# A hybrid encoder layer on one core: the first rows loaded ahead of the constants and whole, u's first product in a bank of its own, the final norm's products shared by VectorE and GpSimd

## The chip, the core and the metric

The kernel runs on one core of one Trainium2 chip. The core has five engines with a queue of instructions each: TensorE (PE in the profile, its weight loads PEld), VectorE (DVE), ScalarE (ACT), GpSimd (POOL) and SyncE (SP), which here issues all transfers between memory and the core. The metric is the device time of one execution in microseconds; the median of a few runs is given.

## What is computed

One layer of an encoder over two sequences of 512 tokens and 1024 features (a prompt and a sample), each with a memory of 256 rows of its own. Cut to what matters here:

```
def _layer(x, mem, l, p):
    xn = _rmsnorm(x, p['norm_mix'][l])
    mn = _rmsnorm(mem, p['norm_mem'][l])
    h = xn @ p['w_in'][l]
    u, q, k, v, xq, g = jnp.split(h, IN_SPLITS, axis=-1)
    y_s5 = _s5_branch(u, ...)
    ...
    y_diff = _diff_attention(q, k, v, lam, ...)
    mk, mv = jnp.split(mn @ p['w_mem_kv'][l], 2, axis=-1)
    y_x = _cross_attention(xq, mk, mv)
    ...
    x = x + merged @ p['w_out'][l]
    xn2 = _rmsnorm(x, p['norm_ffn'][l])
    gate, up = jnp.split(xn2 @ p['w_ffn_in'][l], 2, axis=-1)
    return x + (jax.nn.silu(gate) * up) @ p['w_ffn_out'][l]

def _trunk(x, mem, p):
    for l in range(DEPTH):
        x = _layer(x, mem, l, p)
    return _rmsnorm(x, p['norm_final'])
```

DEPTH is 1. The change touches three places: the first step of `mn @ w_mem_kv`, the first columns of `h` (which are `u`, the input of the state-space branch), and the last `_rmsnorm` with `norm_final`.

## The kernel before

Features lie on the 128 partitions, tokens along the free axis: both sequences together are 1024 columns, and 1024 features are 8 blocks (KD) of 128. Every matrix product in full precision is made of three: weight and data are each split into a high part (a rounded copy, made by ACT) and a low part (the rest, made by DVE), and `mm3` multiplies high by high, high by low and low by high into one bank (L134 to L138 are `split`, the products themselves are all recorded at L66). `weight` loads one 128x1024 weight tile `wf` (L146) and splits it into `wh`, `wl`; each of these three tiles has two buffers.

PE writes its sums to banks of 512 columns. There are eight: four in the pool `mm`, taken with `bank()`, and four in the pool `tr`, taken with `aux()`. A bank is given out again in turn, once its last reader is done.

**Start.** The constants `vec` (the scales of all the norms) are loaded first (L118). `NWARM` products of zeros keep PE busy until the first data are there. Then comes the memory product: `w_mk[0]` is loaded in two halves, each split on arrival, and behind each half `mem_part(i)` loads and splits a part of the memory, two blocks of features at a time (`mh`, `ml`, `mt` in the rows; the norm's scale out of `vec` goes in with the split, L137 and L138). Part 0 is loaded in two transfers, one per block (L228), the others in one (L225). `mem_k(h, w)` makes a quarter of the memory's keys, `mem_v(c, w)` a quarter of its values, the values of all four quarters being summed in four banks `ob` of the pool `mm`. Between them ACT and DVE prepare the layer's input: sums of squares, the norm's factor (`factor`: square root on ACT, reciprocal on DVE, then a transpose on PE that spreads the factor over a bank `bc`), and `x_norm`, which makes `xh`, `xl`.

**u.** After `mem_v(3)` the four banks `ob` are copied by ACT (L371, `mf` in the rows). The first product of u takes the next bank of the same pool, which is the first of these four.

**End.** The last 4 of the 22 blocks of the second feed-forward product are done for three groups of columns: all 512 of the first sequence (c = 0), then the first and the second 256 of the other (c = L and c = L + L // 2). For each group and each of the 8 blocks m of features PE makes the product, DVE adds it to `y[m]` (L1315), ACT squares it, and the squares are added up. `final` then takes the norm's factor and scales the 8 blocks: on DVE in one instruction with the scale `norm_final` and the factor read from its bank (L1292), or, for the middle group, on POOL (L1290), which gets the factor as a copy that ACT makes (`b_`, L1287, `acc` in the rows), the scale having been put in by ACT before (L1319). `final` yields after each block, and for the middle group its steps are called between the blocks of the last group. After each two blocks the result is stored (L1295).

The text's order isn't the order of a queue: the library that builds the program places the instructions of each engine itself, within their dependencies. `issue_after(x)` is a tie: what stands in it comes behind instruction x on the same engine.

Of the kernel before, what the change touches and what calls it, by code (L numbers as in the profile page):

```python
# [10 lines left out]
F32 = mybir.dt.float32  # L11
F32R = mybir.dt.float32r
I32 = mybir.dt.int32
AF = mybir.ActivationFunctionType
ALU = mybir.AluOpType
# [4 lines left out]
P = 128  # L20
L = 512
DM = 1024
KD = DM // P
NS = 2
NT = NS * L
# [47 lines left out]
def encoder(ctx: ExitStack, tc: tile.TileContext, a, out):  # L73
    nc = tc.nc
    V, S, PO, PE = nc.vector, nc.scalar, nc.gpsimd, InOrder(tc, nc.tensor)
# [7 lines left out]
    wp = ctx.enter_context(tc.tile_pool(name="wp", bufs=2))  # L83
# [22 lines left out]
    def slot(tag, shape=(P, NT), dt=F32, name="sl"):  # L106
        return pools[tag].tile(list(shape), dt, tag=tag, name=name)

    def bank(tag="mm"):
        return pools[tag].tile([P, 512], F32, tag=tag, name="bk" + tag)  # L110

    def aux():
        return bank("tr")


    ident = cst.tile([P, P], F32, name="ident")
    vec = cst.tile([P, N_VEC], F32, name="vec")
    nc.sync.dma_start(vec, a["vecs"])  # L118
    onec = cst.tile([P, 2], F32, name="onec")
    V.memset(onec, 1.0)  # L120
# [5 lines left out]
    def vcol(name, i=0):  # L126
        o = VEC[name][0] + i
        return vec[:, o : o + 1]


    def split(hi, lo, src, scale=None):

        if scale is None:
            h = S.copy(hi, src)  # L134
            l_ = V.tensor_tensor(out=lo, in0=src, in1=hi.bitcast(F32), op=ALU.subtract)  # L135
        else:
            h = S.activation(out=hi, in_=src, func=AF.Copy, scale=scale)  # L137
            l_ = V.scalar_tensor_tensor(out=lo, in0=src, scalar=scale, in1=hi.bitcast(F32), op0=ALU.mult, op1=ALU.subtract)  # L138
        return h, l_
# [3 lines left out]
    def weight(src, n=DM, tag=None):  # L143
        nonlocal last_w, last_s
        wf = wp.tile([P, DM], F32, tag="wf", name="wf")
        last_w = nc.sync.dma_start(wf[:, :n], src)  # L146
        wh, wl = (slot(tag, dt=F32R, name=n_) if tag else wp.tile([P, DM], F32R, tag=n_, name=n_) for n_ in ("wh", "wl"))
        last_s = split(wh[:, :n], wl[:, :n], wf[:, :n])
        return wh, wl
# [3 lines left out]
    def mm3(outs, wh, wl, xs, k, nk):  # L153

        nonlocal last_mm
        ws = slice(k * P, (k + 1) * P)
        for s, (xh, xl) in enumerate(xs):
            PE.matmul(outs[s], wh[:, ws], xh, start=(k == 0), stop=False)
            PE.matmul(outs[s], wh[:, ws], xl, start=False, stop=False)
        for s, (xh, xl) in enumerate(xs):  # L160
            last_mm = PE.matmul(outs[s], wl[:, ws], xh, start=False, stop=(k == nk - 1))
# [33 lines left out]
    def factor(ss, n, nt=4, bias=epsc):  # L195

        rs = rp.tile([P, 4], F32, tag="rs", name="rs", bufs=4)
        S.activation(out=rs[:, :nt], in_=ss[:, :nt], func=AF.Sqrt, scale=1.0 / n, bias=bias)
        V.reciprocal(rs[:, :nt], rs[:, :nt])
        bc = aux()  # L200
        for t in range(nt):
            PE.transpose(bc[:, t * P : (t + 1) * P], rs[:, t : t + 1].broadcast_to([P, P]), ident)
        return rs, bc
# [16 lines left out]
    ml = [slot("it" if i else "mem", [P, 2, L], F32R, f"ml{i}") for i in range(4)]  # L220

    def mem_part(i):
        mt_ = slot("ld", [P, 2, L], name="mt")
        if i:
            nc.sync.dma_start(mt_, a["memT"][:, 2 * i : 2 * i + 2, :])  # L225
        for j in range(2):
            if i == 0:
                nc.sync.dma_start(mt_[:, j], a["memT"][:, j, :])  # L228
            split(mh[i][:, j, :], ml[i][:, j, :], mt_[:, j, :], scale=vcol("norm_mem", 2 * i + j))

    last_sq = None
# [62 lines left out]
    def queued():  # L294

        return tc.issue_after(last_w.ins)
# [9 lines left out]
    for _ in range(NWARM):  # L306
        PE.matmul(idle[:, :P], pad_r[:, :P], pad_r[:, :P], start=True, stop=True)


    wf = wp.tile([P, DM], F32, tag="wf", name="wf")  # L310
    wh, wl = (wp.tile([P, DM], F32R, tag=n_, name=n_) for n_ in ("wh", "wl"))
    for i in range(2):
        hs = slice(i * L, (i + 1) * L)
        nc.sync.dma_start(wf[:, hs], a["w_mk"][0][:, hs])
        split(wh[:, hs], wl[:, hs], wf[:, hs])
        mem_part(i)
    mw = [(wh, wl)]
    mem_part(2)
    mem_part(3)
    mw.append(weight(a["w_mk"][1]))  # L320
    with queued():
# [29 lines left out]
    with yielding(last_s):  # L351
        x_norm(0, norm[0], range(5, 8))
        _, bc = factor(ss1, DM)
# [12 lines left out]
    with tc.issue_after(last_s[0].ins):  # L366
        mfs = []
        for s in range(NS):
            mfs.append(slot("ld", [P, 2, L], name="mf"))
            for j in range(2):  # L370
                S.copy(mfs[s][:, j], ob[2 * s + j])  # L371
    uw.append(weight(a["w_in"][1]))
    with queued():
        next(s5)
    for s in range(NS):
# [8 lines left out]
    for t2 in range(2):  # L384
        if t2:
            uw = [weight(a["w_in"][2 + t]) for t in range(2)]
        us = [slot("ld", [P, T, NS, NC], name="ut") for _ in range(2)]
        for s in range(NS):
            for t in range(2):
                o = bank()  # L390
                for k in range(KD):
                    mm3([o], *uw[t], [x_of(k, s)], k, KD)
                S.copy(us[t][:, :, s, :], o.rearrange("p (j c) -> p j c", c=NC))
        for t in range(2):
            nc.sync.dma_start(uD[(2 * t2 + t) * P : (2 * t2 + t + 1) * P], us[t])
# [121 lines left out]
    with behind():  # L517
# [3 lines left out]
        rs_, bc = factor(sums(a["memN"], "ld"), DM)  # L521
# [4 lines left out]
    for t in range(4):  # L526
        o = proj(a["w_glu"][t], zh, zl, 4)
# [37 lines left out]
    ld = lp.tile([P, 2], F32, tag="ld", name="ld", bufs=1)  # L565
# [9 lines left out]
    for i in range(4):  # L575
        th, tl = slot("mkv", [P, 2, L], F32R, "mkvh"), slot("mkv", [P, 2, L], F32R, "mkvl")
        mt_ = slot("ld", [P, 2, L], name="mt")
# [108 lines left out]
    for i in range(-AHEAD, len(steps) + 1):  # L686
        if i + AHEAD < len(steps):
            h, s, lt = steps[i + AHEAD]
# [12 lines left out]
        if 0 <= i < len(steps):  # L701
            h, s, lt = steps[i]
# [8 lines left out]
        if i > 0 and steps[i - 1][2] == 3:  # L711
            h, s, _ = steps[i - 1]
            pTh, pTl = pT.pop((h, s))
            oo = bank("oo")
            hs = slice(h * P, (h + 1) * P)
# [109 lines left out]
    s0, ss, osb = {}, {}, {}  # L825
# [72 lines left out]
    n = len(steps)  # L898
# [226 lines left out]
    for i in range(KFF):  # L1125
# [16 lines left out]
        if i == 0:  # L1142
            for s in range(NS):
                _, bc = rstd(accs[s], DM)
# [3 lines left out]
        with ExitStack() as es_:  # L1148
# [3 lines left out]
            for s, gf, up in ((0, gf0, up0), (1, gf1, up1)):  # L1152
                cs = slice(s * L, (s + 1) * L)
# [17 lines left out]
    y = [y2[m // 2][:, m % 2] for m in range(KD)]  # L1171
# [46 lines left out]
    for v, (m, lo_, hi_) in enumerate(VISITS):  # L1218
        ps = [bank() for _ in range(6)] + [aux()]
        for p in range(lo_, hi_):  # L1220
# [12 lines left out]
            for p_, (nm, o) in zip(ps, SEVEN):  # L1233
                wh, wl = w[nm]
# [40 lines left out]
    def column_sums(acc, n):  # L1275
        ss = aux()
        ones(ss, acc, n, True, True)
        return ss

    def final(ss, c0, n):  # L1280

        cs = slice(c0, c0 + n)
        _, bc = factor(ss, DM, n // P)
        if c0 == L:

            b_ = new_acc()
            S.copy(b_[:, :n], bc[:, :n])  # L1287
        for m in range(KD):
            if c0 == L:
                PO.tensor_tensor(out=y[m][:, cs], in0=y[m][:, cs], in1=b_[:, :n], op=ALU.mult)  # L1290
            else:
                V.scalar_tensor_tensor(out=y[m][:, cs], in0=y[m][:, cs], scalar=vcol("norm_final", m), in1=bc[:, :n],  # L1292
                                       op0=ALU.mult, op1=ALU.mult)
            if m % 2 == 1:
                nc.sync.dma_start(out[c0 // L, :, m - 1 : m + 1, c0 % L : c0 % L + n], y2[m // 2][:, :, cs])  # L1295
            yield
# [3 lines left out]
    for c, n in ((0, L), (L, L // 2), (L + L // 2, L // 2)):  # L1300
        acc = new_acc()
        for m in range(KD):
            if c == 0:
                wsrc = a["w_fo"][m, :, 2 * NPAIR * P :]
                if m == 0:
                    kept.append(weight(wsrc, nb * P))
                else:
                    wf = wp.tile([P, DM], F32, tag="wf", name="wf")[:, : nb * P]
                    nc.sync.dma_start(wf, wsrc)
                    split(k0[:, m - 1], k1[:, m - 1], wf)  # L1310
                    kept.append((k0[:, m - 1], k1[:, m - 1]))
            o = bank()[:, :n]
            for k in range(nb):
                mm3([o], *kept[m], [(ah[k][:, c : c + n], al[k][:, c : c + n])], k, nb)
            V.tensor_tensor(out=y[m][:, c : c + n], in0=y[m][:, c : c + n], in1=o, op=ALU.add)  # L1315
            if c + n < NT or m < KD - 3:
                sum_sq(acc, y[m][:, c : c + n], m == 0, n, V if m == KD - 1 else PO)
                if c == L:
                    S.activation(out=y[m][:, c : c + n], in_=y[m][:, c : c + n], func=AF.Copy, scale=vcol("norm_final", m))  # L1319
                elif c > L:  # L1320
                    for _ in range((0, 0, 1, 2, 5)[m]):
                        next(end)
                continue

            if m == KD - 3:
                ss = aux()
                ones(ss, acc, n, start=True)
            sq = rp.tile([P, L], F32, tag="nsq", name="nsq", bufs=2)
            S.square(sq[:, :n], y[m][:, c : c + n])
            ones(ss, sq, n, stop=(m == KD - 1))  # L1330
        end = final(ss if c + n == NT else column_sums(acc, n), c, n)
        if c != L:
            for _ in end:
                pass
# [422 lines left out]
```

## Time and profile before

| | us |
|---|---|
| median of three runs (lowest, highest) | 1606.04 (1605.71, 1608.06) |
| the profiled execution | 1609.13 |
| its span | 1607.4 |
| PE busy | 1587.6 (99%) |
| DVE busy | 1164.2 (72%) |
| ACT busy | 638.6 (40%) |
| POOL busy | 560.7 (35%) |
| mean granted clock of PE | 0.998 |

The page and the queries show one profiled execution. A row of the order in time reads: start, duration, engine, line, operation, output <- inputs, shapes, number of instructions merged, and in brackets how long the engine was idle before and who released it. "SPq" is SP's issue of a transfer, not the transfer itself. Rows of waits read: who waited, for whom, microseconds in total, times, the longest. `bkmm` and `bktr` are banks of the two pools. Where rows of a GB/s line are shown, the window is cut into 40 equal slices.

### The profile page before, as it was taken

Reading aid. Unit: us, or ns where it says so; the run is one execution under the profiler, and the core shown is the slowest. Engines: PE = TensorE matmul, PEld = TensorE weight load, DVE = VectorE, ACT = ScalarE, POOL = GpSimd, SP = SyncE. Lnnn points to the kernel's source line nnn. Section 1 sums busy time; section 2 is a strip of 40 time slices with the busy share of each in tenths; the row PEclk is TensorE's granted clock in tenths of the full one; section 3 lists DMA queues with packets and bytes.
Section 4 is the critical chain, followed back from the end, with each engine's and each line's share of the span. In section 5 each row is a group of like instructions: output and inputs, shape, how many; then the busy total and the mean of one; then the engine's idle time right before and its main releaser. Section 6 shows DMA issues by size and latency. Waiting matters only on the chain.

```text
span 1607.4 us, 21636 instructions
## 1 busy us (share of the span) xinstructions
PE 1587.6 (99%) x7842; PEld 1314.0 (82%) x7842; DVE 1164.2 (72%) x1853; ACT 638.6 (40%) x1142; POOL 560.7 (35%) x452
## 2 busy tenths in 40 slices
PE   9999999999999999999999999999999999999997
PEld 7888788887898779777878887888888888788887
DVE  7976997067774666766454668888889877898764
ACT  6644313265552355564123434233323233233333
POOL 0010100000333221300343367666656655644563
PEclk9999999999999999999999999999999999999999
DMA  9544523676763111135354532333332223885322
GB/s 357 179 158 151 166 100 123 178 259 211 255 222 112 41 59 40 58 131 176 134 184 137 153 103 90 125 120 131 118 117 107 92 79 128 325 333 187 107 66 105
DMA packets 105035, 237.86 MB, mean 148 GB/s; under 512 B 13536, under 2 KB 45024, under 8 KB 104928
## 3 DMA queue, kind: packets, MB, share of 16 engines
q1 hardware_dynamic: 104928, 236.47, 43.2%
q8 instruction: 62, 1.02, 0.3%
q14 instruction: 45, 0.37, 0.1%
HBM read 165.16 MB, written 71.27 MB: 147 GB/s over the span
## 4 chain that ended last, share of the span: by engine, by line
PE 85%; DVE 4%; issue 4%; DMA 3%; POOL 3%; ACT 1%; SPq 0%; DVEq 0%; POOLq 0%; ACTq 0%
PE bkmm L66 73%; PE bktr L66 2%; PE bksc L66 2%; PE bkoo L66 2%; PE bktr L69 2%; DMA yt<-bD 1%; PE bktr L1591 1%; POOL mg L788 1%; POOL ts L964 1%; DVE tl L135 1%; POOL y L1244 1%; PE bktr L1562 1%; PE bktr L1651 0%; PE bktr L1650 0%; PE bktr L1652 0%
## 5 line engine op out<-in xcount | busy, mean ns | idle before, releaser
L66 PE MATMUL bkmm<-xh,wh 128*128 128x512 f32 x640 | 255.7, 399 | 0.9 <-ACT mf L371 0.9
L66 PE MATMUL bkmm<-xh,wl 128*128 128x512 f32 x640 | 250.7, 392 | 0.0
L66 PE MATMUL bkmm<-xl,wh 128*128 128x512 f32 x640 | 250.5, 391 | 0.0
L66 PE MATMUL bkmm<-th,wh 128*128 128x512 f32 (+1 forms) x621 | 241.1, 388 | 0.7 <-ACT th L134 0.7
L66 PE MATMUL bkmm<-tl,wh 128*128 128x512 f32 (+1 forms) x621 | 241.2, 388 | 0.6 <-DVE tl L135 0.6
L66 PE MATMUL bkmm<-th,wl 128*128 128x512 f32 (+1 forms) x621 | 240.8, 388 | 0.0
L134 ACT CAST wh<-wf 128x1024 fp32r<-128x1024 f32 (+1 forms) x134 | 117.8, 879 | 185.3 <-PE bkmm L66 162.7
L135 DVE TENSOR_TENSOR wl<-wf,wh 128x1024 fp32r<-128x1024 f32 (+1 forms) x134 | 148.9, 1111 | 51.7 <-ACT wh L134 47.1
L66 PEld LDWEIGHTS bkmm<-xh,wh 128*128 128x128 f32 x640 | 120.3, 188 | 31.6 <-issue 7.9
L66 PE MATMUL bkmm<-th,w 128*128 128x512 f32 x432 | 142.0, 393 | 2.0 <-DVE up L1093 0.8
L66 PEld LDWEIGHTS bkmm<-xh,wl 128*128 128x128 f32 x640 | 120.2, 188 | 26.7 <-issue 1.3
L66 PEld LDWEIGHTS bkmm<-xl,wh 128*128 128x128 f32 x640 | 120.4, 188 | 22.2 <-issue 0.4
L66 PEld LDWEIGHTS bkmm<-tl,wh 128*128 128x128 f32 x621 | 116.6, 188 | 25.1 <-DVE tl L135 1.3
L66 PEld LDWEIGHTS bkmm<-th,wh 128*128 128x128 f32 x621 | 116.6, 188 | 24.8 <-ACT th L134 0.8
L66 PEld LDWEIGHTS bkmm<-th,wl 128*128 128x128 f32 x621 | 116.5, 188 | 24.0
L455 POOL TENSOR_TENSOR raw<-raw 128x128 f32<-128x128 f32 x28 | 14.8, 529 | 290.0 <-DVE hl L138 256.3
L1156 POOL TENSOR_TENSOR up<-up,acc 128x512 f32<-128x512 f32 x44 | 84.1, 1933 | 68.0 <-DVE up L1093 68.0
L66 PEld LDWEIGHTS bkmm<-th,w 128*128 128x128 f32 x432 | 81.0, 188 | 24.3 <-DVE up L1093 3.7
L1155 ACT ACTIVATE ac<-gf 128x512 f32<-128x512 f32 x44 | 27.8, 633 | 179.2 <-DMA aD<-ac 91.4
L788 POOL TENSOR_TENSOR mg<-mg,gl 128x1024 f32<-128x1024 f32 x16 | 43.5, 2720 | 140.8 <-DVE gl L784 140.8
L549 ACT ACTIVATE e<-bksc,nb 128x512 f32<-128x512 f32 (+1 forms) x96 | 58.8, 615 | 80.7 <-DVE nb L544 51.7
L66 PE MATMUL bkmm<-tl,w 128*128 128x512 f32 x216 | 84.2, 390 | 0.0
(640 smaller groups left out, 3590.5 us busy)
## 6 DMA issues: line engine op xcount, KB each, us to landing
wf<-in_w_in SPq DMA_DIRECT2D x40, 512.0 KB, 3.8
wD<-hl SPq DMA_DIRECT2D x28, 512.0 KB, 2.9
w<-wD SPq DMA_DIRECT2D x28, 512.0 KB, 4.6
gD<-gt SPq DMA_DIRECT2D x24, 512.0 KB, 2.8
gl<-gD SPq DMA_DIRECT2D x24, 512.0 KB, 3.3
wf<-in_w_fg SPq DMA_DIRECT2D x22, 512.0 KB, 3.6
wf<-in_w_fu SPq DMA_DIRECT2D x22, 512.0 KB, 3.6
aD<-ac SPq DMA_DIRECT2D x22, 512.0 KB, 2.8
```

Source lines behind the costliest of these rows:

```text
L66: return self.put(self.eng.matmul(*args, **kw))
L69: return self.put(self.eng.transpose(*args, **kw))
L134: h = S.copy(hi, src)
L135: l_ = V.tensor_tensor(out=lo, in0=src, in1=hi.bitcast(F32), op=ALU.subtract)
L549: last_x = S.activation(out=e, in_=sc, func=AF.Exp, bias=nb, scale=scale, accum_out=sm)
L788: PO.tensor_tensor(out=mg[m], in0=mg[m], in1=gt, op=ALU.add)
L964: PO.tensor_tensor(out=t_[:, 2], in0=b22, in1=b12, op=ALU.subtract)
L1155: last_t = S.activation(out=ac[:, cs], in_=gf, func=AF.Tanh, scale=0.5)
L1156: PO.tensor_tensor(out=up, in0=up, in1=accs[s], op=ALU.mult)
L1244: PO.tensor_tensor(out=yv, in0=yv, in1=c_, op=ALU.add)
L1562: PE.matmul(kp[64 * hf : 64 * hf + 48, g * 144 : (g + 1) * 144], l_[:, 2 * hf + g, :], o_[:, 4 * g4 + 2 * hf + g, :], start=(l_ is lr48), ...
L1591: PE.matmul(ps[:, g * P : (g + 1) * P], w_[:, gg * P : (gg + 1) * P], u_[:, 8 * o + gg, :], start=True, stop=True)
```

## The change

Three edits in one. At the start, part 0 of the memory is loaded in one transfer, issued ahead of `vec`, and `w_mk[0]` is loaded and split whole, by `weight`. For u, the first product takes a bank of the pool `tr`, given out before the two steps of the state-space branch that follow in the text. At the end, `final` is told which blocks are `ready` (already scaled by ACT, to be multiplied on POOL) and which are `late` (on DVE, behind the last add). The middle group: blocks 0 and 1 on DVE, 4 to 7 on POOL, 2 and 3 late on DVE. The last group: blocks 0 to 2 on POOL with a copy of the factor, 3 to 7 on DVE. The first group stays as it was.

```diff
@@ -115,6 +115,8 @@
     vec = cst.tile([P, N_VEC], F32, name="vec")
+    mt0 = slot("ld", [P, 2, L], name="mt")
+    nc.sync.dma_start(mt0, a["memT"][:, 0:2, :])
     nc.sync.dma_start(vec, a["vecs"])
@@ -220,12 +222,12 @@
     def mem_part(i):
-        mt_ = slot("ld", [P, 2, L], name="mt")
-        if i:
+        if i == 0:
+            mt_ = mt0
+        else:
+            mt_ = slot("ld", [P, 2, L], name="mt")
             nc.sync.dma_start(mt_, a["memT"][:, 2 * i : 2 * i + 2, :])
         for j in range(2):
-            if i == 0:
-                nc.sync.dma_start(mt_[:, j], a["memT"][:, j, :])
             split(mh[i][:, j, :], ml[i][:, j, :], mt_[:, j, :], scale=vcol("norm_mem", 2 * i + j))
@@ -306,15 +308,9 @@
-    wf = wp.tile([P, DM], F32, tag="wf", name="wf")
-    wh, wl = (wp.tile([P, DM], F32R, tag=n_, name=n_) for n_ in ("wh", "wl"))
-    for i in range(2):
-        hs = slice(i * L, (i + 1) * L)
-        nc.sync.dma_start(wf[:, hs], a["w_mk"][0][:, hs])
-        split(wh[:, hs], wl[:, hs], wf[:, hs])
-        mem_part(i)
-    mw = [(wh, wl)]
+    mw = [weight(a["w_mk"][0])]
+    mem_part(0)
+    mem_part(1)
     mem_part(2)
@@ -370,6 +366,7 @@
     uw.append(weight(a["w_in"][1]))
+    u_bank = aux()
     with queued():
         next(s5)
@@ -387,7 +384,7 @@
             for t in range(2):
-                o = bank()
+                o = bank() if t2 or s or t else u_bank
                 for k in range(KD):
@@ -1277,20 +1274,25 @@
-    def final(ss, c0, n):
+    def scaled(m, c0, n):
+        S.activation(out=y[m][:, c0 : c0 + n], in_=y[m][:, c0 : c0 + n], func=AF.Copy, scale=vcol("norm_final", m))
+
+    def final(ss, c0, n, ready=(), late=()):
 
         cs = slice(c0, c0 + n)
         _, bc = factor(ss, DM, n // P)
-        if c0 == L:
-
+        if ready:
             b_ = new_acc()
             S.copy(b_[:, :n], bc[:, :n])
-        for m in range(KD):
-            if c0 == L:
+        for m in (0, 1, 4, 5, 6, 7, 2, 3) if late else range(KD):
+            if m in ready:
                 PO.tensor_tensor(out=y[m][:, cs], in0=y[m][:, cs], in1=b_[:, :n], op=ALU.mult)
             else:
-                V.scalar_tensor_tensor(out=y[m][:, cs], in0=y[m][:, cs], scalar=vcol("norm_final", m), in1=bc[:, :n],
-                                       op0=ALU.mult, op1=ALU.mult)
+                with ExitStack() as es_:
+                    if m in late:
+                        es_.enter_context(tc.issue_after(last_add.ins))
+                    V.scalar_tensor_tensor(out=y[m][:, cs], in0=y[m][:, cs], scalar=vcol("norm_final", m), in1=bc[:, :n],
+                                           op0=ALU.mult, op1=ALU.mult)
             if m % 2 == 1:
                 nc.sync.dma_start(out[c0 // L, :, m - 1 : m + 1, c0 % L : c0 % L + n], y2[m // 2][:, :, cs])
             yield
@@ -1312,13 +1314,13 @@
-            V.tensor_tensor(out=y[m][:, c : c + n], in0=y[m][:, c : c + n], in1=o, op=ALU.add)
+            last_add = V.tensor_tensor(out=y[m][:, c : c + n], in0=y[m][:, c : c + n], in1=o, op=ALU.add)
             if c + n < NT or m < KD - 3:
                 sum_sq(acc, y[m][:, c : c + n], m == 0, n, V if m == KD - 1 else PO)
-                if c == L:
-                    S.activation(out=y[m][:, c : c + n], in_=y[m][:, c : c + n], func=AF.Copy, scale=vcol("norm_final", m))
-                elif c > L:
-                    for _ in range((0, 0, 1, 2, 5)[m]):
+                if (c == L and m >= 4) or (c > L and m < 3):
+                    scaled(m, c, n)
+                if c > L:
+                    for _ in range((0, 0, 1, 2, 3)[m]):
                         next(end)
                 continue
@@ -1328,7 +1330,12 @@
-        end = final(ss if c + n == NT else column_sums(acc, n), c, n)
+        if c > L:
+            for _ in end:
+                pass
+
+        ready = range(4, KD) if c == L else range(3) if c > L else ()
+        end = final(ss if c + n == NT else column_sums(acc, n), c, n, ready, (2, 3) if c == L else ())
```

## The prediction

> **What bounds the kernel now.** I read the page first, then the waits of PE, then the two ends of the run in order of time, because all three edits sit at places where PE does not work.
>
> ```profile
> span 1607.4 us, 21636 instructions
> PE 1587.6 (99%) x7842; PEld 1314.0 (82%) x7842; DVE 1164.2 (72%) x1853; ACT 638.6 (40%) x1142; POOL 560.7 (35%) x452
> PE bktr L66 <- ACT mh L137: 1.1, 1, 1.1
> PE bkmm L66 <- ACT mf L371: 0.9, 1, 0.9
> PE bktr L66 <- DVE ml L138: 0.5, 2, 0.3
> 339.81 20.17 PE bkmm L66 x89
> ```
>
> PE is busy 1587.6 of 1607.4 us, so 19.8 us is all that an edit which removes no matmul can touch. The three waits are all that PE has in its first 130 us, beside the one for its first idle products. The edits aim at 1.1 + 0.5 (memory rows at the start), 0.9 (u's first product), and the stretch after PE's last product. Between 55 and 130 us it has none, and the last row, from the chain that ended last, is one run of PE's products over 20 us: that chain goes through PE, not through a transfer or another engine with a time of its own. I therefore let a gain at the start count in full at the end.
>
> **The start.** SP issues the loads in this order, and ACT and PE follow:
>
> ```profile
> 0.74 0.39 SPq L118 DMA_DIRECT2D vec<-in_vecs  x1
> 1.18 0.42 SPq L314 DMA_DIRECT2D wf<-in_w_mk  x1
> 1.65 0.90 SPq L228 DMA_DIRECT2D mt<-in_memT  x2
> 2.59 0.43 SPq L314 DMA_DIRECT2D wf<-in_w_mk  x1
> 3.06 1.45 SPq L225 DMA_DIRECT2D mt<-in_memT  x3
> 3.92 0.62 ACT L134 CAST wh<-wf 128x512 fp32r<-128x512 f32 x1 [1.46 <-DMA wf<-in_w_mk]
> 5.09 0.72 ACT L137 ACTIVATE mh<-mt,vec 128x512 fp32r<-128x512 f32 x1 [0.55 <-DMA mt<-in_memT]
> 8.19 0.62 ACT L134 CAST wh<-wf 128x512 fp32r<-128x512 f32 x1 [0.65 <-DMA wf<-in_w_mk]
> 9.43 3.81 ACT L137 ACTIVATE mh<-mt,vec 128x512 fp32r<-128x512 f32 x6 [0.62 <-DMA mt<-in_memT]
> 1.18 6.05 PE L66 MATMUL bktr<-pad_r 128*128 128x128 f32 x30 [1.18 <-DVE pad_r L82]
> 6.98 0.48 PE L66 MATMUL bktr<-mh,wh 128*128 128x512 f32 x1
> 10.99 0.50 PE L66 MATMUL bktr<-ml,wh 128*128 128x512 f32 x1 [0.29 <-DVE ml L138]
> 11.55 0.39 PE L66 MATMUL bktr<-mh,wh 128*128 128x512 f32 x1
> GB/s 0 0 0 0 0 5 56 36 130 369 355 341 273 225 273 259 225 143 246 300 314 321 341 369 335 369 341 382 341 355 341 410 423 410 423 423 382 389 430 376
> 13.19 1.06 ACT L134 CAST wh<-wf 128x1024 fp32r<-128x1024 f32 x1
> 14.28 1.22 DVE L135 TENSOR_TENSOR wl<-wf,wh 128x1024 fp32r<-128x1024 f32 x1
> ```
>
> PE's idle matmuls keep it until about 7.0, so its first real product cannot begin earlier whatever lands first. Row blocks go by in threes (three products of about 0.23 each, 0.69 a block); the last block that waits is the third, whose low part comes at 10.99, and the fourth starts at 11.55. That 11.55 is my mark. The edit removes two issues ahead of the second memory part: before, `vec`, half a weight, two rows, half a weight, then the part at 3.06; after, the first part whole, `vec`, the weight whole, then the part. Issues are 0.45 apart, so the whole weight is issued third, at about 1.65 (its second half is at 2.59), and the second memory part at about 2.1 instead of 3.06: some 0.95 earlier each. The bytes ahead of each are the same: 20 KB + 4 x 262 KB = 1.07 MB until the whole weight is in. Summing the GB/s row (0.3 us a slice) that amount has passed at 6.3, yet the second half's cast starts at 8.19.
>
> What is given up: the weight no longer comes in halves, so the first product needs the cast of all 1024 columns (1.06) and the first low product another 1.22 of DVE, where a 0.62 cast was enough. The landing of the whole weight is not in the trace. Bounds: no earlier than now, 8.17 (the queue is full anyway); or bytes through at 6.3 - 0.94 = 5.4 and the lag of the first half (0.6, 3.9 against about 3.3 in the same row), 6.0. I take the issue advance with the present lag, 8.17 - 0.94 = 7.2, because the second half is the transfer with the same bytes ahead of it.
>
> At 7.2: cast to 8.3, low part to 9.54. PE: first product 8.32, second 8.55, third 9.56 (it waits for the low part), then without a gap: second block 9.79, third 10.48 (its rows land at 9.40 - 0.95 = 8.45, high part 9.2, low part behind the weight's on DVE, 10.3), fourth 11.17. Gain 11.55 - 11.17 = **0.4**. At 6.0 the same steps give a fourth block at 9.9, gain 1.6; at 8.17 they give 12.1, loss 0.5. The later casts (13.19) stand behind the same six ACT operations and move with them. The smaller costs: `vec` is issued 0.45 later, but its first reader on the path is the first memory row, which lands no sooner; ACT and DVE convert that row inside PE's idle matmuls (done by about 5.8).
>
> **u's first product.**
>
> ```profile
> 52.52 1.98 PE L66 MATMUL bkmm<-wl,mh 128*128 128x512 f32 x8
> 55.37 0.50 PE L66 MATMUL bkmm<-xh,wh 128*128 128x512 f32 x1 [0.88 <-ACT mf L371]
> 54.74 0.57 ACT L371 COPY mf<-bkmm 128x512 f32<-128x512 f32 x1
> 49.01 3.38 DVE L255 SCALAR_TENSOR_TENSOR xt<-xt,vec,bktr 128x512 f32<-128x512 f32 x5 [0.45 <-PE bktr L69]
> 53.51 1.22 DVE L135 TENSOR_TENSOR wl<-wf,wh 128x1024 fp32r<-128x1024 f32 x1
> ```
>
> PE ends at 54.50 and waits 0.88 for the copy that empties the bank. With a bank of the other pool that wait goes; the bank's last readers are long done. What is late next is the low part of u's weight, at 54.73 on DVE. It is wanted by the third product, 0.46 behind the first: with PE at 54.50, at 54.96, in time. With the start's 0.4, PE is there at 54.1 and the third product at 54.6 would wait 0.15, unless DVE is earlier too; DVE's only wait here (0.45) is for PE, so it may be. The two edits together: at least 55.37 - (54.73 - 0.46) = 1.1, at most 0.4 + 0.88 = 1.3. I take **1.15**. The bank is held until u's first copy, some 6 us; three others are left in its pool. The second product's bank is then the first one emptied, 5.5 us after it is needed now: no cost.
>
> **The end.**
>
> ```profile
> 1597.65 0.42 DVE L1315 TENSOR_TENSOR y<-y,bkmm 128x256 f32<-128x256 f32 x1 [2.12 <-PE bkmm L66]
> 1599.57 0.17 DVE L199 RECIPROCAL rs<-rs 128x2 f32<-128x2 f32 x1 [1.50 <-ACT rs L198]
> 1600.33 3.22 DVE L1292 SCALAR_TENSOR_TENSOR y<-y,vec,bktr 128x256 f32<-128x256 f32 x8 [0.59 <-PE bktr L69]
> 1596.73 5.50 POOL L1290 TENSOR_TENSOR y<-y,acc 128x256 f32<-128x256 f32 x8 [3.14 <-ACT acc L1287]
> 1596.28 0.37 ACT L1287 COPY acc<-bktr 128x256 f32<-128x256 f32 x1 [0.24 <-PE bktr L69]
> 1600.89 0.37 SPq L1295 DMA_DIRECT2D out_y<-y  x1
> 1603.58 0.46 SPq L1295 DMA_DIRECT2D out_y<-y  x1
> GB/s 0 0 194 399 376 382 67 0 0 83 365 365 376 388 376 387 393 366 393 387 377 382 393 376 377 399 376 387 382 376 393 360 45 0 0 0 0 0 0 0
> out_y<-y SPq DMA_DIRECT2D x6, 256.0 KB, 2.5
> L1595 DVE COPY st<-bktr x16: 678/686/686, 134.4 to 162.3; 64x504 f32<-64x504 f32 x16
>   ACT st L1594: 3.5, 6
> ```
>
> The last eight products on DVE take 3.22 (0.40 each), POOL's eight of the block before 5.50 (0.69 each) and reach to 1602.23. But the end is not set by DVE alone. The GB/s row covers 1600.0 to 1607.4 in slices of 0.185: from 1601.75 to 1605.95 the stores run without a gap at about 380 GB/s. That is six stores of 0.69 = 4.1 us, begun 0.86 after the issue at 1600.89. The last issue, 1603.58, alone would be through at 1603.58 + 0.86 + 0.69 = 1605.1. So DVE's saving is worth only what the stores' queue lets through.
>
> After: the middle block gives two products to DVE at once, four to POOL (1596.7 to 1599.5 instead of 1602.2), and two to DVE behind the last add (1598.07 to 1598.9, inside the 1.50 that DVE waits for the reciprocal; without that cover they would cost 0.8). The last of its four stores, issued near 1599.5, is through at 1599.5 + 0.86 + 0.69 = 1601.1. The last block: a copy on ACT of 0.37, three products on POOL, five on DVE. The copy and DVE's products read one bank. The row L1595 shows such a pair: ACT copies one half of the partitions of a bank and DVE the other, both from the same products, and DVE waited for ACT 6 times. So DVE starts at 1600.33 + 0.42 = 1600.75 and ends at 1602.75; POOL 1600.8 to 1602.85. Stores: fifth and sixth rows at 1601.98, then 1602.45, 1602.9, 1603.4 (0.46 apart); the stream starts at 1602.84 and ends 2.76 later, 1605.6. Gain 1605.95 - 1605.6, **0.3**. Without the wait between the readers 1605.2, gain 0.7; with the stores in the text's order (pair 0-1 first, at 1602.2) 1605.8, gain 0.1.
>
> The Trainium skill (PSUM — Partial Sum Buffer, section "PSUM bank collisions raise a hardware error") says that two engines may not access one bank in the same partitions at once, reads against reads included. That speaks against this part: by it the 0.7 is out of reach and 0.3 stands; the row above agrees, 3.5 us in 6 waits.
>
> **Sum:** 1.15 + 0.3 = 1.45. The profiled execution took 1609.13 (span 1607.4, 1.7 around it) and would take 1607.7. It lies 3.1 above the median of the runs, 1606.04; the same saving there gives **1604.6**.
>
> **Rivals.** (a) *All parts add up*: the weight lands at 6.0 and DVE's chain up to u's weight moves with PE, which its one wait for PE speaks for, that it has only this 0.45 to give against: 1.6 + 0.88 + 0.7 = 3.2, time 1602.8. (b) *The gains are absorbed*: the weight lands at 8.17 (-0.5) and the stores keep the text's order: -0.5 + 0.88 + 0.1, time 1605.6. (c) *Slower: the whole weight stands ahead of the memory rows in ACT's queue.* In the text the split of the weight comes first, as the half did (3.92 before 5.09). If it keeps that place and lands at 8.17, the rows' high part waits behind it: cast to 9.25, first row 9.97, its low part on DVE behind the weight's (10.5) at 11.25, and the fourth block at about 13.3 instead of 11.55. PE loses 1.7, u's edit returns 0.88, the end 0.3: 1606.6. It decides from the point where the cast of the weight begins ahead of both rows; against it speaks that the rows are now issued first. (d) *Order elsewhere*: the queues do not follow the text (the store issued at 1600.89 or just after belongs to whichever product is ready), so the edits can shift orders far away. A new wait like the two largest of PE, 1.7 and 1.3, costs 3.0:
>
> ```profile
> PE bksc L66 <- DVE ql L135: 1.7, 1, 1.7
> PE bkmm L66 <- DVE gl L784: 1.3, 2, 0.9
> ```
>
> time 1607.6, and more if it repeats; such waits could also vanish.
>
> **How the numbers follow.** Forecast 0.50 (its own range 1603.4 to 1605.8); (a) 0.22; (b) 0.10; (c) 0.08; (d) 0.10. A change of 0.2% is 3.2 us, about what a measurement of this kernel can tell from none; so faster is below 1602.8, slower above 1609.3. Faster: half of (a) and a third of (d), 0.11 + 0.03 = 0.14. Slower: the rest of (d) and little of (c), 0.07 + 0.01 = 0.08. Within: 0.78. The range takes in (a) with most of its spread, (b) and (c): 1602.0 to 1607.2.
>
> **What would show it.** Start: SP's third issue is the whole weight at about 1.65; its cast begins at 7.2 (6.0 to 8.2) and behind both memory rows; PE's fourth block starts near 11.2. u: no wait on the copy of `mf`; the first product at 54.2. End: DVE's last five products begin about 0.4 after the transposes, behind ACT's copy; the stores stop 0.3 earlier measured from PE's last product. I am wrong if the whole weight lands no earlier than its second half does now, if PE meets a wait past 130 us that is not in the list of before, or if the stores end later after PE's last product than now.

## The result and the profile after

The changed kernel takes 1618.63 us (median of 6 runs, 1617.35 to 1622.75), the kernel before 1608.01 (6 runs, 1605.71 to 1609.67): a ratio of 1.0071, interval 1.0061 to 1.0082. It is slower by some 11 us, where 1604.6 was forecast and 1607.2 was the upper end of the range. The profiled execution took 1621.13, 12.0 more than the one of before.

The page of the changed kernel, and below its rows PE's waits before 130 us, without the one for its first idle products (who waited for whom, total, times, longest):

```profile
span 1619.4 us, 21622 instructions
PE 1590.9 (98%) x7842; PEld 1315.6 (81%) x7842; DVE 1165.9 (72%) x1853; ACT 636.3 (39%) x1141; POOL 555.5 (34%) x451
PE bktr L1537 <- DVE cxi L1525: 3.9, 1, 3.9
PE bktr L66 <- ACT wh L136: 2.8, 1, 2.8
PE bkmm L66 <- ACT mf L367: 2.0, 2, 1.1
PE bkmm L66 <- DVE wl L137: 1.1, 1, 1.1
PE bktr L66 <- DVE wl L137: 0.5, 1, 0.5
PE bktr L1537 <- DVE cxr L1525: 0.5, 1, 0.5
```

PE has the same 7842 products, 3.3 us more busy time (1590.9 against 1587.6) and 8.7 us more idle time (1619.4 - 1590.9 = 28.5 against 19.8). Idle time is in these waits: before 130 us they add up to 10.8, against 2.5 before. More busy time for the same products means slower products; the rows below show them where the granted clock is below 1.00.

The start, in order of time, and under it the windows (length, busy time and number of instructions of PE, PEld, DVE, ACT, POOL, granted clock, DMA share, GB/s):

```profile
4.51 1.33 ACT L139 ACTIVATE mh<-mt,vec 128x512 fp32r<-128x512 f32 x2 [2.04 <-DMA vec<-in_vecs]
7.92 1.04 ACT L136 CAST wh<-wf 128x1024 fp32r<-128x1024 f32 x1 [2.08 <-DMA wf<-in_w_mk]
9.02 0.50 PE L66 MATMUL bktr<-mh,wh 128*128 128x512 f32 x1 [2.77 <-ACT wh L136]
10.28 0.50 PE L66 MATMUL bktr<-mh,wl 128*128 128x512 f32 x1 [0.53 <-DVE wl L137]
12.77 0.63 PE L66 MATMUL bktr<-mh,wh 128*128 128x512 f32 x1
8.00:10.00 2.00, 0.73 (x2) 0.30 (x2) 1.00 (x1) 1.76 (x3) 0.00 (x0) 1.00 1.01 389
10.00:12.00 2.00, 1.72 (x6) 1.40 (x7) 2.00 (x4) 2.00 (x4) 0.00 (x0) 0.77 0.96 383
12.00:14.00 2.00, 2.00 (x6) 1.57 (x5) 2.00 (x4) 1.96 (x3) 0.00 (x0) 0.50 0.94 319
```

The memory rows are ready early (ACT has converted both by 5.84), but the whole weight's cast starts at 7.92. PE stands idle for 2.77 us, and then its granted clock is 0.77 and 0.50. The fourth block begins at 12.77, before at 11.55.

u. Here is what PE does with u's products, and where the one on the new bank (`bktr<-xh,wh`) has gone:

```profile
57.43 0.50 PE L66 MATMUL bkmm<-xh,wh 128*128 128x512 f32 x1 [0.88 <-ACT mf L367]
59.30 0.50 PE L66 MATMUL bkmm<-xh,wh 128*128 128x512 f32 x1 [1.13 <-ACT mf L367]
78.53 1.06 PE L1537 MATMUL bktr<-ident,cxr 128*128 128x128 f32 x8 [0.49 <-DVE cxr L1525]
80.71 0.50 PE L66 MATMUL bkmm<-xh,wl 128*128 128x512 f32 x1 [1.11 <-DVE wl L137]
91.70 1.06 PE L1537 MATMUL bktr<-ident,cxi 128*128 128x128 f32 x8 [3.91 <-DVE cxi L1525]
92.42 1.07 ACT L1538 COPY wb<-bktr 128x512 f32<-128x512 f32 x2 [3.88 <-PE bktr L1537]
92.52 0.48 PE L66 MATMUL bktr<-xh,wh 128*128 128x512 f32 x1
93.53 0.63 PE L66 MATMUL bktr<-xh,wh 128*128 128x512 f32 x1
93.96 0.63 PE L66 MATMUL bktr<-xl,wh 128*128 128x512 f32 x1
```

The product that was to start near 54 us is not the first but the last of its group: 92.52, directly behind the last transposes (L1537) of the state-space step, whose two banks ACT copies from 92.42 and from 92.90 on (the row of L1538). The wait for ACT's copy that it was to remove, 0.88, is still there, since another product of u takes its place in PE's queue, and a second one follows. The four waits from 59.30 on add up to 6.64. From 93.1 on the products follow each other at 0.43 instead of 0.23: half the clock again, for 3 us. The late product also holds back what comes after it: its weight lies in one of two buffers, and u's fourth weight is cast only at 99.64, released by this product, where the kernel before has it at 79.09. So PE had no further product of u to put into its wait of 3.91.

The ledger of the two profiled executions: u's first product begins 57.43 - 55.37 = 2.06 later; the four waits 6.64; some eight products behind the last of them at 0.43 instead of 0.23, 1.7; together 10.4. A row well behind this stage (ACT's first `sg`) stands at 359.8 before and at 370.3 after, 10.5 later, so nearly all is lost by then. The other 1.5 is spread over the rest of the run; no single wait carries it, and its cause stays open.

The end, DVE, ACT, POOL and the stores of the last block:

```profile
1609.61 0.42 DVE L1317 TENSOR_TENSOR y<-y,bkmm 128x256 f32<-128x256 f32 x1
1609.94 0.86 DVE L1294 SCALAR_TENSOR_TENSOR y<-y,vec,bktr 128x256 f32<-128x256 f32 x2
1612.45 0.37 ACT L1286 COPY acc<-bktr 128x256 f32<-128x256 f32 x1 [0.95 <-PE bktr L69]
1612.85 2.05 DVE L1294 SCALAR_TENSOR_TENSOR y<-y,vec,bktr 128x256 f32<-128x256 f32 x5 [1.16 <-ACT acc L1286]
1612.89 2.10 POOL L1289 TENSOR_TENSOR y<-y,acc 128x256 f32<-128x256 f32 x3 [1.45 <-ACT acc L1286]
1614.14 1.98 SPq L1297 DMA_DIRECT2D out_y<-y  x4
```

This is as it was worked out: the two late products lie inside DVE's wait, and the five last ones wait for ACT's copy of the same bank. From the last add to the end of the span it is 1619.4 - 1609.61 = 9.79, before 1607.4 - 1597.65 = 9.75: the 0.3 that was forecast here does not show.

### The profile page after: what moved, and what is told of

It is laid out like the page before. It is cut to its first block, busy times and chain, and to the rows that moved or that the text cites. A ratio compares the mean times of both kernels' runs of the same rounds, so it can differ in the third digit from the quotient of the medians.

```text
span 1619.4 us, 21622 instructions
## 1 busy us (share of the span) xinstructions
PE 1590.9 (98%) x7842; PEld 1315.6 (81%) x7842; DVE 1165.9 (72%) x1853; ACT 636.3 (39%) x1141; POOL 555.5 (34%) x451
## 4 chain that ended last, share of the span: by engine, by line
PE 84%; DVE 6%; DMA 3%; issue 2%; POOL 2%; ACT 2%; SPq 0%; POOLq 0%; DVEq 0%; ACTq 0%
PE bkmm L66 72%; PE bktr L66 3%; PE bksc L66 2%; PE bkoo L66 2%; PE bktr L69 2%; PE bktr L1598 1%; DVE tl L137 1%; POOL ts L961 1%; DVE wl L137 1%; PE bktr L1569 1%; DMA acc<-in_w_fo 0%; DVE w L140 0%; PE bktr L1659 0%; PE bktr L1658 0%; PE bktr L1657 0%
## 5 line engine op out<-in xcount | busy, mean ns | idle before, releaser
L66 PE MATMUL bkmm<-xh,wl 128*128 128x512 f32 x632 | 246.8, 391 | 1.1 <-DVE wl L137 1.1
L66 PE MATMUL bkmm<-xl,wh 128*128 128x512 f32 x632 | 247.0, 391 | 0.0
```

The source lines that it names most:

```text
L66: return self.put(self.eng.matmul(*args, **kw))
```

## The experiments

Two theories. **B**: u's bank is given out again, in the order of the text, to transposes that stand in the text between its taking and its use; this is the 8 to 9 us. **S**: the late start puts everything behind it out of step with DVE, which is nearly full up to 100 us. Times are medians, with the ratio to the kernel before, which ran beside them on the same chip (1607.77 to 1608.1 in these sessions), and its interval. The ratio is not the quotient of the two medians and can differ from it by about a thousandth; where the two disagree, go by the interval.

**u's bank back.**

```diff
-    u_bank = aux()
-                o = bank() if t2 or s or t else u_bank
+                o = bank()
```

> The change with u's first product back on the next bank of its pool; start and end stay changed. Theory B (the bank is given out again): in the text the bank is taken ahead of the transposes of the state-space step, which take twelve banks of the same pool of four, so that the same bank goes to the fourth, eighth and twelfth of them and u's product stands behind all of these, at 92.5 us instead of about 55. It then costs about 8 to 9 us, and this kernel takes about 10 less than the changed one's excess over the start: some 2 us over the kernel before. Theory S (the late start does it: the first weight comes late, and everything behind it is out of step with VectorE, which is nearly full from 40 to 100 us): the excess stays at 8 or more.

Measured: 1610.35, ratio 1.0006 (0.9995 to 1.0017). The late start is still in it, most of the 10.6 us are not. S falls. So u's edit is what costs them; how its bank does it is the question of the later runs.

**The start back.** The lines of the start as they were before; u's bank and the end stay changed.

> The change with the start as before (weight in halves, constants first); u's bank and the end stay changed. Theory B: 2 us less than the changed kernel, with the first product of u on the shared bank still near 90 us: 8 to 10 over the kernel before. Theory S: within 2 us of the kernel before.

Measured: 1621.37, ratio 1.0072 (1.0057 to 1.0088). Both theories were too kind: nothing is won back. u's edit alone, with the end, costs as much as all three. The windows from 55 to 110 us of the two traces show one reason why the losses don't add, the first row of the changed kernel, the second of this run:

```profile
55.00:110.00 55.00, 47.30 (x230) 37.52 (x229) 44.46 (x47) 23.97 (x59) 3.28 (x5) 0.97 0.32 115
```

```profile
55.00:110.00 55.00, 49.16 (x226) 39.74 (x227) 42.28 (x44) 21.70 (x55) 3.27 (x5) 0.91 0.30 105
```

PE comes earlier to the same stalls, is idle 1.9 us less, and then runs at 0.91 instead of 0.97 over these 55 us, which is about 3.3 us.

**The end alone**, on the kernel before.

> The kernel before with the new end alone. Theory E (the products on VectorE wait for ScalarE's copy of the same bank, and the stores set the end): the time from the last add to the end stays at 9.75 us within 0.2, and the time within 0.5 us of the kernel before. Rival (the new tie behind the last add and three products on GpSimd cost something on the path): 1 us or more slower. My forecast's own step: 0.3 faster.

Measured: 1608.35, ratio 0.9998 (0.9989 to 1.0008). No effect that can be told, and the time from the last add to the end is 1607.3 - 1597.52 = 9.78: theory E holds. Its trace has the start of the kernel before, unchanged, and yet:

```profile
12.00:14.00 2.00, 2.00 (x7) 1.57 (x7) 2.00 (x4) 2.00 (x4) 0.00 (x0) 0.59 1.04 342
14.00:16.00 2.00, 2.00 (x6) 1.55 (x6) 1.95 (x6) 0.45 (x1) 0.00 (x0) 0.55 1.04 394
```

The clock falls here too, at the same place where the trace of before has 1.00. So with the old start it falls in some executions. u's first product then begins at 57.14, where the trace of before has 55.37: of the 2.06 in my ledger the old start loses 1.77 too when its clock falls.

**A pool of its own for u's bank**, so that nothing else can take it.

```diff
-    open_banks(mm=4, tr=4)
+    open_banks(mm=4, tr=3, ub=1)
-    u_bank = aux()
+    u_bank = bank("ub")
```

> The change, but u's bank is in a pool of its own, so that nothing else can take it (the pool of four shrinks to three in this stage). Theory B: u's first product starts as soon as the memory's values end, at about 57 less 0.9 us, the four stalls between 57 and 92 us go, and the kernel takes about 1 us more than the one before (start +2, u -0.9). Theory S: 8 or more over the kernel before, as the start is still late.

Measured: 1614.44, ratio 1.0036 (1.0022 to 1.005). The stage from 55 to 110 us is now full (PE busy 55.00 of 55.00; u's first product starts at 56.31), so B is right about the stalls, and S is wrong again. The time is some 5 us above what B gave for this run: 200 us later two new waits stand in PE's rows:

```profile
255.69 0.50 PE L66 MATMUL bkmm<-xh,wl 128*128 128x512 f32 x1 [1.53 <-DVE wl L137]
268.80 0.50 PE L66 MATMUL bkmm<-xh,wl 128*128 128x512 f32 x1 [1.94 <-DVE wl L137]
```

Behind the second the clock is 0.62 and 0.53 from 269 to 273 us.

**A bank of the same pool, taken at the same line and used at once.** The changed kernel with the first product and its copy moved up in the text.

```diff
+    us0 = [slot("ld", [P, T, NS, NC], name="ut") for _ in range(2)]
     u_bank = aux()
+    for k in range(KD):
+        mm3([u_bank], *uw[0], [(xh[k][:, 0:L], xl[k][:, 0:L])], k, KD)
+    S.copy(us0[0][:, :, 0, :], u_bank.rearrange("p (j c) -> p j c", c=NC))
     with queued():
         next(s5)
```

> The changed kernel with u's first product, and the copy that empties its bank, moved in the text directly behind the taking of the bank, ahead of the state-space step; pools, start and end as changed. Theory B (the bank is given out again in the order of the text): the same bank of the same pool now serves at once, u's first product starts where the memory's values end, and the four stalls between 57 and 92 us are gone: at least 6 us less than the changed kernel. What is left over the kernel before is the start's excess and what the plan makes of later stages, as in the run with a pool of its own (5.8 over): 1 to 6 us. Rival (a bank of this pool is slow or held for another reason): as the changed kernel, within 2 us.

Measured: 1608.43, ratio 1.0005 (0.9996 to 1.0015), 10.2 below the changed kernel.

```profile
55.88 0.39 PE L66 MATMUL bktr<-xh,wh 128*128 128x512 f32 x1
```

The product is on a bank of the pool `tr` and starts without a wait, where the changed kernel had it at 92.52. The waits at the start apart (0.98 and 0.53), PE has none before 130 us, and none at 255. The pool as such was not at fault. Nor is the place in the text alone: in the kernel before and in the run with a pool of its own the product stands behind the same transposes in the text and starts at 55.37 and 56.31. It takes both, the shared pool and a use behind twelve others that take banks of it.

One detail of B is not borne out. If u's bank were that of the twelfth transposes, the product would have to wait for ACT's copy of it. In the changed kernel that copy begins at 92.90, the product at 92.52; in the run with the start back they begin at 92.40 and 92.02. Which bank the product gets, the traces don't show. They would fit a pool that gives out its banks in the order of first use, u's as the thirteenth; no run separates this from other rules.

**The pool of its own alone**, on the kernel before (the first hunk above, and `bank("ub")` for u's first product).

> The kernel before, with u's first product in a pool of its own and nothing else. My forecast's step: the wait of 0.88 goes, 0.9 us faster. Theory P (with that wait gone the planner orders the stage behind it differently; in the run with the own pool PE then waited 1.5 and 1.9 us for the low part of a weight at 255 and 268 us, and its clock fell to half behind that): the two waits are there again, and the kernel is 2 to 4 us slower than the one before. If the waits of that run came from the changed start, they are absent here.

Measured: 1612.11, ratio 1.0022 (1.0012 to 1.0032). The two waits are back, at 253.50 and 266.61 (1.55 and 1.94), without the changed start:

```profile
253.50 0.50 PE L66 MATMUL bkmm<-xh,wl 128*128 128x512 f32 x1 [1.55 <-DVE wl L135]
266.61 0.50 PE L66 MATMUL bkmm<-xh,wl 128*128 128x512 f32 x1 [1.94 <-DVE wl L135]
```

The clock stays at 1.00 behind them here. They come with the pool of three, or with the order that it leads to, which the run above with four banks does not have. Which of the two, no run shows.

**More idle products at the start**: `NWARM` 22 instead of 15, in the changed kernel with u's bank back.

> The changed kernel with u's bank back, and 22 idle products at the start instead of 15. Theory C (with the changed start PE stands idle between its idle products and the first cast weight, and the clock then runs at half for some 3 us; all three traces with this start show it): the idle products reach to about 9 us, PE's granted clock stays at 1.00 from 8 to 18 us, and the kernel takes 1.5 us less than with 15, so no more than the kernel before. Rival (the clock falls by chance, or the idle products delay the first real one): the clock falls again, or no gain.

Measured: 1611.24, ratio 1.0017 (1.0007 to 1.0026). The clock does what was expected, 1.00 in every window from 8 to 18 us (the changed kernel had 0.77 and 0.50):

```profile
10.00:12.00 2.00, 1.47 (x7) 1.24 (x7) 2.00 (x4) 2.00 (x5) 0.00 (x0) 1.00 0.92 341
12.00:14.00 2.00, 2.00 (x10) 1.61 (x9) 2.00 (x4) 2.00 (x4) 0.00 (x0) 1.00 0.88 316
57.96 0.57 ACT L367 COPY mf<-bkmm 128x512 f32<-128x512 f32 x1
58.59 0.79 PE L66 MATMUL bkmm<-xh,wh 128*128 128x512 f32 x1 [3.37 <-ACT mf L367]
```

The time does not follow: the first copy of `mf` now stands behind seven copies of the state-space step in ACT's queue instead of one, and u waits 3.37 for it instead of 0.88. Behind that wait the clock is 0.50 from 58 to 64 us. Idle products at 1 us moved an order at 57 us.

**More idle products, the kernel before otherwise.**

> The kernel before with 22 idle products instead of 15; the start otherwise as it was. Theory C: the first real products are held back by some 2 us, from 7.0 to about 9, but the last block that waits for its rows (11.0) is not, so PE's end does not move; the clock, which fell in one trace of this start and not in two others, stays up: 0 to 1 us faster, with less spread. Rival (the idle products only delay): up to 2 us slower.

Measured: 1606.55, ratio 0.9991 (0.9982 to 1.0000). The clock is 1.00 in every window from 8 to 18 us, u's wait is 0.9 as before. A gain of about 1.5 by the medians, at the edge of what can be told.

**The start alone**, on the kernel before.

> The kernel before with the changed start alone. Theory C: the first product waits for the cast of the whole weight, at about 8.5 to 9.1 instead of 6.6 to 7.0; the clock falls to half between 10 and 14 us in every run, where before it falls in some: 1 to 2 us slower. My forecast's step: 0.4 faster.

Measured: 1609.13, ratio 1.0008 (0.9998 to 1.0017). The sign is as expected, but the interval takes in 1: from 0.3 faster to 2.7 slower. Its cast starts at 7.60, PE waits 1.37 for it, and the clock is 0.50 from 10 to 12 us. What the start costs is clearer in the traces, at the point where PE is done with the memory product (the start of u's first product less its wait):

| start | traces | us |
|---|---|---|
| old, clock stays at 1.00 | 3 | 54.09 to 54.49 |
| old, clock falls (the end alone) | 1 | 56.27 |
| changed, clock falls | 5 | 55.88 to 56.55 |
| changed, 22 idle products, clock stays | 1 | 55.22 |
| old, 22 idle products, clock stays | 3 | 53.85 to 54.13 |

The late weight costs about 1 us, and the fall of the clock, which all five traces of the changed start with 15 idle products have, about another (0.7 to 1.3). The old start loses about 2 when its clock falls, in one of its four traces.

**The rows first, the weight in halves**, with 22 idle products.

> The kernel before with the first memory part loaded whole and ahead of the constants, the weight still in halves, and 22 idle products. Theory: the rows are not what is late, so that against the run with 22 idle products alone (1606.5) nothing is gained: within 1 us of it. Rival (rows first helps, and only the whole weight spoilt it): 1 us faster than that run.

Measured: 1609.44, ratio 1.0011 (1.0001 to 1.0021). The time is inconclusive on its question: the last product that waits for rows starts at 10.19 (10.74 in the next run, which has the old loads and as many idle products), so the rows do come earlier, and PE is done with the memory product at 53.74, 0.1 to 0.4 ahead of the last row of the table above. But u has the wait of 3.37 again, with the copies in the order of the run with 22 idle products on the changed start, and the clock at 0.50 behind it.

**What is left of the idea**: on the kernel before, u's first product moved up as above and 22 idle products; then the same with the changed end.

> The kernel before with two edits: u's first product on a bank of the other pool, taken, used and emptied in the text ahead of the state-space step, and 22 idle products. Theory: the wait of 0.88 at u is gone, the clock stays up at the start, and the plan of the later stages keeps no new stall (the run with the same u edit on the changed start had none): 2 us faster than before. Rival (the planner gives the gain back elsewhere, as it did with the own pool): no faster than the run with 22 idle products alone, 1606.5.

> The same two edits with the changed end as well (start as before). Theory E: the end is worth 0.1 to 0.3 us, below what can be told: within 1 us of the run without it. Rival: 1 us or more apart, which would show that the end's edit changes the plan ahead of it.

Measured: 1605.6, ratio 0.9985 (0.9976 to 0.9995), and 1605.24, ratio 0.9984 (0.9975 to 0.9993). Both are faster than the two kernels of the change, by 2.2 and 2.5 us against the one before. The end makes no difference that can be told. Nor can it be told what u's edit adds to the 22 idle products, which alone gave 0.9991: the intervals overlap. In the traces u's first product starts at 54.13 in both and at 54.73 with the idle products alone. PE's waits before 130 us in the first of them, all of them:

```profile
PE bktr L66 <- DVE pad_r L82: 1.2, 1, 1.2
PE bktr L66 <- DVE ml L138: 0.3, 1, 0.3
```

## Why the prediction was wrong

**The step that failed** is in the part on u: "With a bank of the other pool that wait goes; the bank's last readers are long done", and "three others are left in its pool". I asked who had used the bank before and not who gets it next. Between the line that takes `u_bank` and the lines that use it stand two steps of the state-space branch, and they take twelve banks of the same pool of four. Since u's product is written behind them in the text and shares their pool, it comes behind all twelve on the chip: 92.52, right after the last transposes. The wait of 0.88 was not removed, and four waits of 6.64 and a slowed clock were added. Three runs each take one condition away, and the product starts at 55.9 to 57.3: u's bank back in its old pool, a pool of its own, and the use moved up. The last gave 10.2 of the 10.6 back. That the twelve delay it is shown; by which rule the pool hands out its banks is not. The prediction had all it needed for this: the profile lists the transposes on `bktr`, and the diff shows the order.

**The start** went the other way, by one step that failed and a term that was missing. The whole weight's cast was put at 7.2, the present 8.17 less the advance of the issue. The issue did come 0.93 earlier (1.66 against 2.59), but the six traces with this start have the cast at 7.42, 7.60, 7.79, 7.92, 7.97 and 8.19. The cast of the second half starts at 7.14 to 8.19 in the seven traces that load as before; the 8.19 that I started from is the latest of them. So the whole weight comes no earlier than the half did, which I had named as a sign of being wrong. Why is open; the DMA engines are busy 95% of the time or more from 6 to 12 us, with either start. The missing term is the clock: PE idle until the cast, then about half speed for some 3 us in each of the five traces that have this start and 15 idle products. I had the idle time in my own steps (7.0 to 8.3) and costed it as idle time only. My opening premise, that only the 19.8 us of idle time can be touched, left out the same thing: PE's busy time rose by 3.3 us with the same products. By its own run the start costs up to 2.7 us, by the traces about 2 against an old start whose clock stays up, where I had a gain of 0.4 and a loss of 0.5 as the bound.

**The end** was right in its mechanism: DVE began behind ACT's copy, 0.40 after it (1612.45 to 1612.85), POOL with it, the late products were hidden. The 0.3 was not measurable; the span says 0.0, the run of the end alone a ratio of 0.9998, with about a thousandth to either side. The row of L1595, which I took to agree with the rule on banks, is not a case of it: there the two engines read different partitions. It shows only that they wait for each other in this program, as they do here.

**The rivals.** (c) named a slower start by its order on ACT; the order was the good one (both rows first, at 4.51), and the loss came all the same. (d), that orders shift far away, was the nearest: it happened in four runs (at 255 us with a pool of three, at 57 us with rows first and more idle products), each worth 2.5 to 3.5 us of waiting, in three of them with a stretch at about half clock behind. But in the changed kernel itself the loss is not an accident of the plan, it follows from the text. My chance of 0.08 for slower came almost wholly from that rival, and for another reason than the one that held.

## What to carry to other kernels

A bank taken early from a shared pool was not held for its user here: ask who takes the next turns between the line that takes it and the line that uses it, and put the two side by side, or the user may wait for all who come between. Cost idle time of PE near the start, or behind any stall, with the clock after it, and check a removed wait by whether the instruction that waited has really moved up. In a kernel whose queues a planner orders, measure each edit alone and the sum again: edits worth 1 us here moved waits of 2 to 3.5 us hundreds of instructions away.

## What the runs showed of the hardware

An idle gap of PE of 1.0 to 2.8 us, with sparse products around it, was followed by about 3 us at a granted clock of 0.50 to 0.77, in windows of 2 us, in all five traces with the changed start and 15 idle products; with the old start it fell in one trace (0.59 and 0.55 from 12 to 16 us) and stayed at 1.00 in three others. The waits of 3.91 at 88 us and of 3.37 at 55 us were followed by 0.50 too. The Trainium skill (TensorE: Matmul & The Clock Gate, section "What's actually happening") puts the fall at an idle window of about 3.4 us that runs free of the program. That it varies from run to run agrees with the traces; the gaps at the start were shorter than that window, though PE was busy for only part of the time around them (0.73 to 0.96 of the 2 us from 8 to 10 us). Seven more idle products kept the clock at 1.00 from 8 to 18 us in all five kernels that had them.

Two engines that read one bank went one after the other here: DVE's five products start when ACT's copy ends, 0.40 behind its start (1612.45 and 1612.85), though both only read. The wait is in the program; whether the chip needs it no run here shows.
